# Order of weight splits and query steps in a windowed attention layer

## The chip, the cores and the metric

The kernel runs on one core of one Trainium2 chip. The metric is the device time of one launch in microseconds (us). One core has TensorE (PE: matmuls and transposes; PEld: its weight loads), VectorE (DVE), ScalarE (ACT), GpSimd (POOL), SyncE (SP, which here issues the DMAs), and 16 DMA engines. All engines share an on-chip memory (SBUF); matmuls write to accumulation banks (PSUM).

## The reference, cut to what matters

A network of two blocks on 512 tokens of width 1024: a retention layer, a windowed attention layer, and then a mixer, cross attention and MLP layers. The change lies in the windowed attention layer alone:

```
def swa_layer(x, g_norm, w_in, g_q, sinks, w_out, k_band, v_band, bias, mask):
    proj = rmsnorm(x, g_norm) @ w_in
    q, gate = jnp.split(proj, [SWA_Q_WIDTH], axis=-1)
    q = rmsnorm(q.reshape(b, nb, BLOCK, SWA_KV_HEADS, SWA_GROUP, SWA_HEAD_DIM), g_q)
    scores = jnp.einsum('bnqkgd,bnjkd->bnkgqj', q, k_band).astype(jnp.float32)
    scores = scores * (SWA_HEAD_DIM ** -0.5) + bias[None, None]
    scores = jnp.where(mask[None, :, None, None], scores, -jnp.inf)
    sink = sinks.astype(jnp.float32).reshape(1, 1, SWA_KV_HEADS, SWA_GROUP, 1, 1)
    m = jnp.maximum(jnp.max(scores, axis=-1, keepdims=True), sink)
    p = jnp.exp(scores - m)
    p = p / (jnp.sum(p, axis=-1, keepdims=True) + jnp.exp(sink - m))
    o = jnp.einsum('bnkgqj,bnjkd->bnqkgd', p.astype(v_band.dtype), v_band)
    o = o.reshape(b, s, SWA_Q_WIDTH) * jax.nn.silu(gate)
    return x + o @ w_out
```

There are 16 query heads of 64, two key/value heads, and four blocks of 128 tokens; a block sees itself and the block before it.

## The kernel before

**Precision.** A factor is split into two parts of a reduced matmul type, `hi` (a rounded copy, written by ScalarE) and `lo` (the rest, written by VectorE). A product is three matmuls, hi by hi, hi by lo and lo by hi: `mm3`, lines L257 to L259.

**Weights.** All weight matrices come in chunks of 128 x 2048 numbers (1 MB), in one list (`order`) in which they are used. `load` issues the DMA of one chunk into one of two raw buffers (`wtiles`, L251) and splits it into one of the weight buffers. In this layer one of the three weight buffers is held for the keys (`hold`), so that two take turns: the split of chunk n + 1 overwrites chunk n - 1, and can begin when the matmuls of n - 1 have ended. The chunks of `b_w_in` have a norm's factors worked into the split: eight ScalarE instructions (`split_scaled`, L168) and eight VectorE instructions (L169) of 128 x 256. Other chunks are split by two of each (`split`, L159 and L160). `prefetch(n)` loads until n chunks are ready; `chunk(..., ahead=k)` first calls `prefetch(k + 1)` and then takes the next one, so that `ahead=1` loads the chunk behind the one that is taken, and `ahead=0` loads none beyond it.

**The layer's loop.** The heads go in four groups c = 0 to 3, the queries of c being chunk 2c of `b_w_in` and its gate chunk 2c + 1. `q_part(c)` works in two halves of two blocks (b2 = 0, 1): a projection with 256 columns for each block (96 matmuls over both halves), `normed` (a square on ScalarE at L648, a sum at L650 and L652, a power on GpSimd at L285, the scaling at L656), a split into `qx` (L159, L160), eight transposes by PE (L706), and four ScalarE copies of the transposed queries into `oh` and `ol` (L709; the tiles are called swa_oh and swa_ol in rows). It is a generator with three steps: the first half up to the split; the first half's transposes and copies and the second half up to the split; the second half's transposes and copies. `gate_part(c)` has two steps, one for each 128 columns of the gate, with 24 matmuls of 512 columns each and the `silu_gate`. `attend(c, b, bt)` does the scores of one block (L742: eight matmuls, for which the transposed queries of that block must be there), the bias and the softmax; `values` transposes the probabilities (L772), splits them (pTh, pTl) and multiplies by the values, then by the gate (L782). It runs three blocks behind.

**What sets the order.** The program text gives priorities. A planner works out, before the run and by its own estimate of each instruction's time, the order of the instructions on each engine: among those whose inputs and buffers it takes to be ready, the one that stands first in the text. The queues then run in that order. So an instruction that stands late in the text can be queued early if it is ready early. `tc.issue_after(ins)` adds to all instructions that its block makes on the engine of `ins` the condition that they are queued behind `ins`; it adds no wait, and holds nothing on other engines.

Of the kernel before, what the change touches and what calls it, by code (L numbers as in the profile page):

```python
# [17 lines left out]
P = 128  # L18
# [95 lines left out]
class Net:  # L114
# [503 lines left out]
    def swa(self, after):  # L618
        nc, tc, a = self.nc, self.tc, self.a
# [23 lines left out]
        def normed(ps3, nh, b2):  # L643

            nh = 2 * nh
            sq = self.sp.tile([P, 512], F32, tag="sq", bufs=3, name=self.uid("qs"))[:, :nh * 64].rearrange(
                "p (h d) -> p h d", d=64)
            nc.scalar.activation(sq, ps3, AF.Square)  # L648
            ss = self.sp.tile([P, 32], F32, tag="ss", name=self.uid("ss"))[:, :nh]
            nc.vector.tensor_reduce(out=ss, in_=sq, axis=AX.X, op=ALU.add)  # L650
            sv = ss.rearrange("p (b h) -> p b h", b=2)
            nc.vector.scalar_tensor_tensor(  # L652
                out=sv, in0=sv, scalar=1.0 / 64, op0=ALU.mult, op1=ALU.add,
                in1=self.e1[:, 2 * b2:2 * b2 + 2].unsqueeze(2).to_broadcast([P, 2, nh // 2]))
            r = self.pow_col(ss, nh, 0.0)
            nc.vector.tensor_tensor(out=sq, in0=ps3, in1=r.unsqueeze(2).to_broadcast([P, nh, 64]), op=ALU.mult)  # L656
            return sq

        ck = self.chunk("w_kv", 0, ahead=1)
        for b2 in range(2):  # L660
# [19 lines left out]
            for x in range(2):  # L680
                pt = self.bank("ax").rearrange("p (b g t) -> p b g t", b=2, g=2)
# [8 lines left out]

        def q_part(c):

            ck = self.chunk("b_w_in", 2 * c, ahead=1)
            for b2 in range(2):
                ps = self.bank().rearrange("p (b c) -> p b c", b=2)
                for b in range(2):
                    self.tproj(ck, xs, b2 * 2 + b, ps[:, b, :])
                qn = normed(ps.rearrange("p b (h d) -> p (b h) d", d=64), 4, b2)
                qx = p2.tile([P, 8, 2, 64], F32R, tag="qx", name=self.uid("qx"), bufs=1)
                self.split(qx[:, :, 0], qx[:, :, 1], qn)  # L700
                qf = qx.rearrange("p (b h) x d -> p b h (x d)", b=2).bitcast(F32)
                yield
                for b in range(2):
                    pt = self.bank("ax").rearrange("p (h t) -> p h t", h=4)
                    for h in range(4):
                        nc.tensor.transpose(pt[:, h], qf[:, b, h], ident)  # L706
                    t0 = b2 * HALF + b * P
                    for i, t in enumerate((oh, ol)):
                        nc.scalar.copy(t[:, 2 * c:2 * c + 2, t0:t0 + P], pt[:, 2 * i:2 * i + 2])  # L709
            yield  # L710

        def gate_part(c):
            ck = self.chunk("b_w_in", 2 * c + 1, ahead=1)
            sg = sgs[c] = p2.tile([P, 2, S], F32, tag="sg", name=self.uid("swsg"))
            for j in range(2):
                self.silu_gate(self.proj(ck, j, xs, full), sg[:, j, :], rb)
                yield
# [3 lines left out]
        def bias_load(c):  # L721
            bt = p2.tile([P, 2, 2, 256], F32, tag="bias", name=self.uid("bias"))
            v = self.scr[:]
            for g in range(2):
                src = bass.AP(tensor=v.tensor, offset=v.offset + 127 + (8 * g + 2 * c) * 384,
                              ap=[[16 * 384 - 1, P], [384, 2], [1, 256]])
                nc.sync.dma_start(bt[:, g], src)
            return bt
# [34 lines left out]
        def values(c, b, s, sg):  # L763
            w = P if b == 0 else 256
            nj = w // P
            po = self.bank("ax")[:, :256]
            n = 0
            for g in range(2):
                pt = self.bank("ax").rearrange("p (j t i) -> p j t i", j=2, t=2)
                for t in range(2):  # L770
                    for j in range(nj):
                        nc.tensor.transpose(pt[:, j, t, :], s[:, g, t, j * P:(j + 1) * P], ident)  # L772
                pT = [p2.tile([P, 2, 256], F32R, tag=x, name=self.uid(x)) for x in ("pTh", "pTl")]
                src = pt.rearrange("p j t i -> p j (t i)")
                self.split(pT[0][:, :nj], pT[1][:, :nj], src[:, :nj])
                for j in range(nj):
                    self.mm3(po, [z[:, b + 1 - nj + j, g, :] for z in vz], [x[:, j, :] for x in pT],
                             n == 0, n == 2 * nj - 1)
                    n += 1
            u = self.sp.tile([P, 512], F32, tag="sq", bufs=3, name=self.uid("ou"))[:, :256].rearrange("p (t i) -> p t i", t=2)  # L780
            bs = slice(b * P, (b + 1) * P)
            nc.vector.scalar_tensor_tensor(out=u, in0=sg[:, :, bs], scalar=0.5,  # L782
                                           in1=po.rearrange("p (t i) -> p t i", t=2), op0=ALU.mult, op1=ALU.mult)
            self.split(oh[:, 2 * c:2 * c + 2, bs], ol[:, 2 * c:2 * c + 2, bs], u)

        for _ in q_part(0):
            pass
        prev = []
        for c in range(4):
            bt = bias_load(c)  # L790
            g, q = gate_part(c), q_part(c + 1) if c < 3 else iter([None] * 3)
            fill = [(g, g), (), (q,), (q, q)]
            for b in range(NB):
                s = attend(c, b, bt)
                for x in fill[b]:
                    next(x)
                if len(prev) == 3:
                    values(*prev.pop(0))
                prev.append((c, b, s, sgs[c]))
# [627 lines left out]
```

## Time and profile before

| | us |
|---|---|
| median of 3 runs | 1888.41 |
| lowest, highest | 1884.99, 2663.68 |
| the profiled execution, its own time | 1888.0 |
| its span in the profile | 1886.2 |
| granted TensorE clock, mean | 0.997 |

The span reaches from the first to the last instruction; 1.8 us of the profiled execution lie outside it. The highest of the three runs is far from the two others. Times in rows are microseconds from the start of the span, unless marked ns. "Idle before" is the time for which an engine stood still ahead of an instruction, with what ended it. PEclk is the granted TensorE clock as a share of full speed.

### The profile page before, as it was taken

The numbers are of one execution on the slowest core, as the hardware profiler recorded it, in microseconds if no ns is written. First come the engines' busy times: TensorE is split into PE (matmuls) and PEld (weight loads), VectorE is DVE, ScalarE is ACT, GpSimd is POOL, SyncE is SP. The second block draws the span as 40 slices with busy tenths as digits, with TensorE's granted clock in tenths as the row PEclk, the third lists the DMA queues.
The fourth block names the chain that finished last, engine by engine and source line by source line (L and its number), as shares of the span: only waits on it lengthen the run. The fifth ranks groups of instructions, "written<-read, shape, count | busy, mean of one in ns | idle before, by whom it ended". The sixth has DMA issues, their size and how long they took to land.

```text
span 1886.2 us, 25702 instructions
## 1 busy us (share of the span) xinstructions
PE 1856.7 (98%) x10626; PEld 1627.5 (86%) x10626; DVE 1115.2 (59%) x1942; ACT 721.0 (38%) x1338; POOL 40.2 (2%) x51
## 2 busy tenths in 40 slices
PE   8999999999999999999999999999999999999998
PEld 7888888889888988888998888888899898888886
DVE  5564646567887566647556644444595575444445
ACT  5333223245655344434543423223254353233231
POOL 0000000001110000000000000000000000000000
PEclk9999999999999999999999999999999999999999
DMA  7224222213221322223522432322322133223221
GB/s 266 95 84 151 87 95 68 90 51 109 67 68 56 115 68 68 90 67 112 195 75 70 158 108 89 105 97 90 108 83 68 68 112 123 90 89 112 90 90 45
DMA packets 34038, 182.50 MB, mean 97 GB/s; under 512 B 4033, under 2 KB 8705, under 8 KB 14721
## 3 DMA queue, kind: packets, MB, share of 16 engines
q1 hardware_dynamic: 33920, 180.86, 27.9%
q8 instruction: 83, 1.36, 0.3%
q14 instruction: 35, 0.28, 0.0%
HBM read 178.72 MB, written 5.27 MB: 98 GB/s over the span
## 4 chain that ended last, share of the span: by engine, by line
PE 95%; DVE 3%; ACT 1%; DMA 0%; issue 0%; SPq 0%; DVEq 0%; POOLq 0%; POOL 0%; ACTq 0%
PE mm L257 30%; PE mm L259 30%; PE mm L258 30%; PE ax L325 1%; DVE w L160 1%; PE ax L257 0%; PE ax L293 0%; PE ax L258 0%; PE ax L259 0%; PE ax L772 0%; PE mm L742 0%; PE ax L1091 0%; ACT w L168 0%; PE ax L706 0%; PE mm L1222 0%
## 5 line engine op out<-in xcount | busy, mean ns | idle before, releaser
L257 PE MATMUL mm<-xh,w 128*128 128x512 f32 (+1 forms) x1312 | 462.4, 356 | 7.4 <-ACT xh L168 6.6
L258 PE MATMUL mm<-xl,w 128*128 128x512 f32 (+1 forms) x1312 | 463.5, 354 | 0.0
L259 PE MATMUL mm<-xh,w 128*128 128x512 f32 (+1 forms) x1312 | 463.4, 354 | 0.0
L159 ACT CAST w<-raw 128x1024 fp32r<-128x1024 f32 (+1 forms) x284 | 282.8, 1043 | 436.2 <-PE mm L259 269.5
L160 DVE TENSOR_TENSOR w<-raw,w 128x1024 fp32r<-128x1024 f32 (+1 forms) x284 | 337.0, 1216 | 130.6 <-ACT w L159 130.5
L257 PEld LDWEIGHTS mm<-xh,w 128*128 128x128 f32 x1312 | 246.1, 189 | 42.7 <-ACT xh L168 6.6
L259 PEld LDWEIGHTS mm<-xh,w 128*128 128x128 f32 x1312 | 247.3, 189 | 34.4
L258 PEld LDWEIGHTS mm<-xl,w 128*128 128x128 f32 x1312 | 247.3, 189 | 34.3 <-DVE xl L169 0.3
L381 DVE SCALAR_TENSOR_TENSOR x<-x,mm 128x512 f32<-128x512 f32 x192 | 131.5, 685 | 201.3 <-PE mm L259 201.2
L257 PE MATMUL mm<-w,hh 128*128 128x512 f32 x512 | 199.3, 389 | 0.0
L258 PE MATMUL mm<-w,hh 128*128 128x512 f32 x512 | 199.2, 389 | 0.0
L259 PE MATMUL mm<-w,hl 128*128 128x512 f32 x512 | 199.2, 389 | 0.0
L257 PE MATMUL mm<-w,xh 128*128 128x256 f32 x544 | 153.4, 282 | 0.9 <-ACT xh L159 0.4
L259 PE MATMUL mm<-w,xl 128*128 128x256 f32 x544 | 152.7, 281 | 0.2 <-DVE xl L160 0.2
L258 PE MATMUL mm<-w,xh 128*128 128x256 f32 x544 | 152.3, 280 | 0.0
L258 PEld LDWEIGHTS mm<-w,hh 128*128 128x128 f32 x512 | 96.1, 188 | 20.1
L259 PEld LDWEIGHTS mm<-w,hl 128*128 128x128 f32 x512 | 96.1, 188 | 19.9
L257 PEld LDWEIGHTS mm<-w,hh 128*128 128x128 f32 x512 | 96.1, 188 | 19.8
L257 PEld LDWEIGHTS mm<-w,xh 128*128 128x128 f32 x544 | 102.9, 189 | 3.8 <-ACT pre L914 2.3
L1159 DVE TENSOR_TENSOR rl<-rl 128x512 f32<-128x512 f32 (+1 forms) x72 | 45.1, 631 | 100.6 <-ACT rl L1157 100.6
L259 PEld LDWEIGHTS mm<-w,xl 128*128 128x128 f32 x544 | 102.9, 189 | 0.4 <-DVE xl L160 0.4
L258 PEld LDWEIGHTS mm<-w,xh 128*128 128x128 f32 x544 | 102.6, 189 | 0.2
(343 smaller groups left out, 2829.6 us busy)
## 6 DMA issues: line engine op xcount, KB each, us to landing
raw<-in_mlp_w_dram SPq DMA_DIRECT2D x64, 1024.0 KB, 4.9
raw<-in_a_w_in_dram SPq DMA_DIRECT2D x23, 1024.0 KB, 5.1
raw<-in_ml_w_in_dram SPq DMA_DIRECT2D x12, 1024.0 KB, 5.1
raw<-in_a_w_out_dram SPq DMA_DIRECT2D x8, 1024.0 KB, 5.0
raw<-in_b_w_in_dram SPq DMA_DIRECT2D x8, 1024.0 KB, 4.9
raw<-in_xa_wq_dram SPq DMA_DIRECT2D x8, 1024.0 KB, 4.8
raw<-in_mem_w_kv_dram SPq DMA_DIRECT2D x8, 1024.0 KB, 5.1
raw<-in_xa_wo_dram SPq DMA_DIRECT2D x8, 1024.0 KB, 5.0
```

What stands on the lines that cost most here:

```text
L159: nc.scalar.copy(hi, src)
L160: return nc.vector.tensor_tensor(out=lo, in0=src, in1=hi.bitcast(F32), op=ALU.subtract)
L257: mm(o, a[0], b[0], start=first, stop=False)
L258: mm(o, a[0], b[1], start=False, stop=False)
L259: mm(o, a[1], b[0], start=False, stop=last)
L325: nc.tensor.transpose(ps[:, t * P:(t + 1) * P], self.x[:, b, f:f + P], self.c("ident"))
L381: self.nc.vector.scalar_tensor_tensor(out=x, in0=x, scalar=alpha, in1=ps, op0=ALU.mult, op1=ALU.add, **({} if acc is None else {"accum_out ...
L1159: nc.vector.tensor_tensor(out=u, in0=u, in1=u, op=ALU.mult)
```

## The change

In `q_part` and `gate_part` the chunk is taken with `ahead=0`. The next chunk's load is called later: in `q_part(c)` behind the transposes and copies of the first half (so that the gate's weights of c come there), and in `gate_part(c)` at once (the queries' weights of c + 1), in both cases inside `issue_after` the last copy so far, which `self.evac` keeps. And the three steps of `q_part(c + 1)`, which ran one in block 2 and two in block 3 of group c, run one in each of the blocks 1, 2 and 3.

```
 
         def q_part(c):
 
-            ck = self.chunk("b_w_in", 2 * c, ahead=1)
+            ck = self.chunk("b_w_in", 2 * c, ahead=0)
             for b2 in range(2):
                 ps = self.bank().rearrange("p (b c) -> p b c", b=2)
                 for b in range(2):
...
                     for i, t in enumerate((oh, ol)):
-                        nc.scalar.copy(t[:, 2 * c:2 * c + 2, t0:t0 + P], pt[:, 2 * i:2 * i + 2])
+                        self.evac = nc.scalar.copy(t[:, 2 * c:2 * c + 2, t0:t0 + P], pt[:, 2 * i:2 * i + 2])
+                if b2 == 0:
+                    with tc.issue_after(self.evac.ins):
+                        self.prefetch(1)
             yield
 
         def gate_part(c):
-            ck = self.chunk("b_w_in", 2 * c + 1, ahead=1)
+            ck = self.chunk("b_w_in", 2 * c + 1, ahead=0)
+            with tc.issue_after(self.evac.ins):
+                self.prefetch(1)
             sg = sgs[c] = p2.tile([P, 2, S], F32, tag="sg", name=self.uid("swsg"))
...
             g, q = gate_part(c), q_part(c + 1) if c < 3 else iter([None] * 3)
-            fill = [(g, g), (), (q,), (q, q)]
+            fill = [(g, g), (q,), (q,), (q,)]
             for b in range(NB):
```

## Rows read from the trace of the kernel before

**Rows 1.** The page: the span, and busy time, share and instructions of each engine.

```profile
span 1886.2 us, 25702 instructions
PE 1856.7 (98%) x10626; PEld 1627.5 (86%) x10626; DVE 1115.2 (59%) x1942; ACT 721.0 (38%) x1338; POOL 40.2 (2%) x51
```

**Rows 2.** Windows: length, busy time of each engine (instructions), clock, DMA share, GB/s.

```profile
445.46:587.00 141.54, 130.41 (x883) 118.46 (x882) 115.66 (x288) 90.79 (x272) 11.76 (x7) 0.99 0.20 64
587.00:1886.20 1299.20, 1288.88 (x7224) 1122.97 (x7223) 741.08 (x1234) 468.71 (x794) 17.29 (x28) 1.00 0.28 95
```

**Rows 3.** Who waited for whom, PE alone, from 440 to 640.

```profile
PE mm L742 <- ACT swa_oh L709: 7.0, 3, 2.8
PE ax L772 <- DVE pTl L160: 2.0, 2, 1.0
PE ax L706 <- DVE qx L160: 1.2, 3, 0.6
PE ax L257 <- DVE ou L782: 0.5, 1, 0.5
```

**Rows 4.** Timeline of PE: start, length, instruction, count, idle time before.

```profile
485.02 1.03 PE L706 MATMUL ax<-cst,qx 128*128 128x128 f32 x8
488.83 0.74 PE L742 MATMUL mm<-kT,swa_oh 128*128 128x256 f32 x4 [2.77 <-ACT swa_oh L709]
...
490.88 1.09 PE L706 MATMUL ax<-cst,qx 128*128 128x128 f32 x8 [0.37 <-DVE qx L160]
...
530.28 0.74 PE L742 MATMUL mm<-kT,swa_oh 128*128 128x256 f32 x4 [2.74 <-ACT swa_oh L709]
...
531.80 1.97 PE L706 MATMUL ax<-cst,qx 128*128 128x128 f32 x8 [0.31 <-DVE qx L160]
...
571.32 0.74 PE L742 MATMUL mm<-kT,swa_oh 128*128 128x256 f32 x4 [1.44 <-ACT swa_oh L709]
```

**Rows 5.** Timeline of ACT at the first and the third of these waits.

```profile
485.22 3.30 ACT L168 ACTIVATE w<-raw,vec 128x256 fp32r<-128x256 f32 x8 [2.55 <-PE mm L259]
488.42 0.35 ACT L709 CAST swa_oh<-ax 128x256 fp32r<-128x256 f32 x1
...
569.00 1.99 ACT L159 CAST w<-raw 128x1024 fp32r<-128x1024 f32 x2 [1.12 <-PE mm L259]
570.90 0.36 ACT L709 CAST swa_oh<-ax 128x256 fp32r<-128x256 f32 x1
```

**Rows 6.** Windows behind the second wait, columns as in rows 2.

```profile
532.00:534.00 2.00, 2.00 (x11) 2.00 (x11) 1.16 (x2) 1.36 (x4) 0.00 (x0) 0.50 0.84 328
534.00:536.00 2.00, 2.00 (x15) 2.00 (x15) 0.00 (x0) 0.45 (x2) 0.00 (x0) 0.75 0.34 143
```

**Rows 7.** Timeline of PE: first matmuls of the gate projections of c = 0 and 1.

```profile
445.46 0.39 PE L257 MATMUL mm<-xh,w 128*128 128x512 f32 x1
...
474.14 0.39 PE L257 MATMUL mm<-xh,w 128*128 128x512 f32 x1
```

**Rows 8.** Groups by line, 440 to 600: count, busy us, mean ns, idle before.

```profile
L168 ACT ACTIVATE w<-raw,vec 128x256 fp32r<-128x256 f32 x48 | 19.9, 497 | 3.7 <-PE mm L259 3.7
```

**Rows 9.** The chain that ended last, in order of time: start, length, what.

```profile
459.30 0.95 PE mm L742 x8
460.25 0.87 PE ax L706 x8
```

**Rows 10.** Timeline, c = 0, first half: ACT's square, DVE's end of the split.

```profile
439.23 0.60 ACT L648 ACTIVATE qs<-mm 128x512 f32<-128x512 f32 x1 [0.48 <-PE mm L259]
...
444.11 0.68 DVE L160 TENSOR_TENSOR qx<-qs,qx 128x512 fp32r<-128x512 f32 x1
```

**Rows 11.** The page's DMA issues: count, size of each, median us to landing.

```profile
raw<-in_b_w_in_dram SPq DMA_DIRECT2D x8, 1024.0 KB, 4.9
```

**Rows 12.** Timeline, c = 1, first half: the same two instructions as in rows 10.

```profile
467.80 0.60 ACT L648 ACTIVATE qs<-mm 128x512 f32<-128x512 f32 x1 [3.57 <-PE mm L259]
...
479.90 0.68 DVE L160 TENSOR_TENSOR qx<-qs,qx 128x512 fp32r<-128x512 f32 x1
```

## The prediction

> **What bounds the kernel now.** I began with the page's first part: TensorE (PE) is busy 1856.7 us of 1886.2 us, 98%, the other engines 59% and less [rows 1]. All that an edit of order can win is therefore idle time of PE, 29.5 us in the whole program, and the question is how much of it lies in the stage that is changed. The windows answer that: the attention layer's loop over head groups runs from the end of the first query projection (445.46) to about 587; in these 141.54 us PE is busy 130.41, so 11.1 us are idle. The 1299 us behind it hold 10.3 us of idle time and the work before 445.46 the rest; the edit touches neither [rows 1, 2]. PE's list of waits for this stage gives 10.7 of the 11.1 us names: 7.0 us in three waits of the scores (L742) for ScalarE's copies of the transposed queries (L709), 2.0 us for VectorE's second part of the probabilities, 1.2 us in three waits of the query transposes (L706) for the second part of qx, 0.5 us for the gated output [rows 3].
>
> The timeline of PE shows where the three big waits stand: 2.77 us before 488.83, 2.74 us before 530.28 and 1.44 us before 571.32, that is, once at each change of the head group c. The first comes right behind eight query transposes that began at 485.02 [rows 4]. ScalarE's timeline says why. At 485.22, when the gate projection of c = 1 has freed its weight buffer, ScalarE takes the eight slices of the next weights (3.30 us) and only then the copy at 488.42. The third wait is the same with a plain split, 1.99 us before the copy at 570.90 [rows 5]. So the wait is neither for PE nor for VectorE but for a place in ScalarE's queue, and it is taken there by weights that nobody wants yet: a gate uses them, and a whole query projection, some 11 us, stands in front of that gate.
>
> One more cost hangs on the second wait. From 532 to 534 the granted clock is 0.50 of full (1.2 GHz) and from 534 to 536 it averages 0.75, with PE busy throughout; what PE does before the clock falls is the 2.74 us of waiting. That is 0.50 x 2 + 0.25 x 2 = 1.5 us lost [rows 4, 6]. Eight transposes take 1.97 us there and 1.09 us after the first wait, where the clock stays up [rows 4].
>
> **The change part by part.** Nothing is removed or added in computation; each of the eight input chunks is still loaded by one DMA and split by eight ScalarE and eight VectorE instructions. Two things move.
>
> First, the order of the splits. The gate's weights of group c, up to now free to be split as soon as their buffer is free, come behind the four copies of the first two blocks' queries of the same c; the queries' weights of c + 1 come behind the last copies of group c. The edge binds ScalarE's half; VectorE's half needs ScalarE's result and follows. The gate projection of c, which stood ahead of those copies (at c = 1 it runs from 474.14 to 485.02, 10.9 us, while the queries are still being normed [rows 7]), must now stand behind them, so its buffer can't come free in front of them either. That holds for the third wait too: the split in front of it, the output weights, goes into the buffer of the last gate. All three waits of L742 lose their cause: **-6.95 us**. The qx waits (0.37, and with the other two 1.25 us together [rows 3, 4]) come from the same queue, since the ScalarE half of qx stands behind the same split and copies: **-1.25 us**. The clock's drop, which follows the second wait: **-1.5 us**. The other 2.5 us of [rows 3] are waits for VectorE inside the softmax; I let them stand.
>
> The Trainium skill (TensorE: Matmul & The Clock Gate, "Part 1: The HAM clock gate") says that the slow clock is the default and activity lifts it. The trace agrees at the second wait and not at the first, which is as long and shows no drop. If the drop is tied to the wait, the sum below stands; if it is not, it may fall elsewhere and the sum is 1.5 us smaller.
>
> What the delayed split costs is not in the trace, and I bound it. From the last copy of the first half to the first usable slice of the gate's weights lie one ScalarE and one VectorE slice, about 0.4 us each by 3.30 / 8 [rows 5] and 497 ns as the mean of one [rows 8]: 0.9 us. Each slice then feeds three matmuls of 0.23 us (10.9 us / 48 [rows 7]), 0.69 us a slice, so the split stays ahead. In those 0.9 us PE has the scores of blocks 0 and 1 of that group, 0.95 us each [rows 9], which wait for these copies alone. So the gap is near 0 if the order comes out that way, and 4.2 us (the whole split and VectorE's tail, 3.3 + 0.9) if the planner puts something else first. I take 0.5 us for each of c = 1, 2, 3, near the lower end, as the scores stand ahead of the gate in program order: **+1.5 us**. A gain is excluded here: work is made later, not cheaper.
>
> At c = 0 there is no such cover. The gate projection starts at 445.46, without a wait, on weights split beforehand [rows 7]. After the change it needs the copies first: the VectorE half of qx ends at 444.8, 0.7 us after 444.11 [rows 10], eight transposes take 0.87 us [rows 9], two copies of 0.35 us [rows 5] 0.7 us more, the first slice 0.9 us: 447.3 at best. In between PE has these transposes and as many of the keys', 1.7 us together. Bounds 0 and 4.2 us as above; I take **+1.0 us**, nearer the lower, as the matmuls of two blocks' scores can go in as well.
>
> Second, the queries' three steps go to blocks 1, 2, 3 where they stood at 2, 3, 3. A step more or less in a block costs nothing of itself: the same instructions. It moves the half chain (square, sum, power on GpSimd, scaling, split) up by a block, and its transposes from the group's end into the block before. What hides it is the work of PE in between: the second half's projection (48 matmuls of half the gate's width, some 5.5 us [rows 7]), the scores and the values. The weights of q(c + 1) have the whole gate projection of c to be split in. VectorE is no bound: 115.66 of 141.54 us [rows 2]. On the DMA queue each of the loads goes out later in the order, a 1 MB transfer of 4.9 us [rows 11] into the raw buffer of the chunk two before, and the bias transfer of the next group stands behind it; the raw buffer is free a gate projection (10.9 us) earlier, so I cost both at nothing. Without that cover it would be up to 4.9 us for a chunk. GpSimd's queue holds only the powers, and no load passes it.
>
> Sum: -6.95 - 1.25 - 1.5 + 1.5 + 1.0 = -7.2 us. Against the profiled execution, 1888.0 us, that is **1880.8, say 1881 us**. The shown median is 1888.4, the same within 0.4 us; the two lower runs are 1885.0 and 1888.4, so some 3 us is chance.
>
> **The rivals.** *A, the forecast:* 1881 us, 1877 to 1885.
>
> *B, the waits change their name:* PE loses as much to the softmax chain or to late gate weights as it gains at the copies. For it: the order on every engine is worked out by a planner before the run, and the old trace is already full of matmuls of the gate that filled gaps; tied to the copies, they no longer can. Against: the gate is now free exactly where the softmax of a new group starts. Price: 0, 1888 us, 1885 to 1891.
>
> *C, slower: the gate projection is missed as cover of the queries' chain.* From the square to the second part of qx the chain takes 5.5 us when VectorE is free (439.23 to 444.8 [rows 10]) and 12.8 us in the loop (467.80 to 480.6 [rows 12]). Now the gate waits for the whole of it: 12.8 + 0.87 (transposes) + 1.4 (four copies) + 0.9 (slice) = 16.0 us from the end of the first half's projection. As cover remain 5.5 us of the second half, 1.9 us of scores and some 2.3 us of one block's values (eight transposes and twelve matmuls of 0.12, as 0.95 / 8 [rows 9]): 9.7 us. Uncovered 6.3 us, three times 18.9 us, with a clock drop of 1.5 us each in place of one: 18.9 + 3.0 - 8.2 = +13.7 us, **1902 us**. It decides from a chain of about 6.5 us on. Against it: in the long chain stand the splits that now come later, and the step has a higher place in the order.
>
> *D, all idle time of the stage goes, and the drop:* 1888.0 - 11.1 - 1.5 = 1875 us. For it speaks that each head group then has scores and a gate ready together; against it the 2.5 us that wait for VectorE. That the change leaves the waits of L742 as they were is no case of its own: the edge forbids it.
>
> **How the numbers follow.** A 0.50, B 0.25, C 0.15, D 0.10. The likeliest is A: 1881 us. The range must leave out no more than 2 in 10: it reaches from D (1875, less 1) over A and B to the milder half of C (up to +5 us): 1874 to 1893. Faster and slower by 2% means 38 us, about what a measurement of this kernel can tell from no change; that is over three times all idle time of the stage, and nearly three times C. So within 2%: 0.98; slower 0.01, faster 0.01.
>
> **What the changed profile would show.** If the first step is right, PE's waits show no L742 behind L709 of over 0.7 us, and on ScalarE four copies L709 stand ahead of each eight slices L168. If the cost of the delay is right, PE's waits for the split (L257 to L259 of the gate behind L168 or L169) sum to under 3 us, some of it at c = 0 near 446. If C is right, PE idles 3 us and more before each gate projection, with a clock of 0.50 behind it. If B is right, idle time between 445 and 587 stays near 11 us under other names, DVE pTl first. Wrong altogether would be a shift outside this stage, where I expect the stretch behind it to have its length of before.

## The result: slower by 1.0%, and where the time went

The changed kernel takes 1906.9 us (median of five runs, 1904.32 to 1909.29) against 1887.03 us before (median of five runs by now): a ratio of 1.0102, interval 1.0086 to 1.0119. The run of 2663.68 us before is a slow one and left out of the ratio. That is within 2%, but its sign is clear, and it is the other sign than forecast, outside the range of 1874 to 1893. The profiled execution took 1905.86 us. Its page answers to [rows 1]:

```profile
span 1904.1 us, 25709 instructions
PE 1866.9 (98%) x10626; PEld 1633.7 (86%) x10626; DVE 1117.5 (59%) x1942; ACT 719.7 (38%) x1338; POOL 40.0 (2%) x51
```

TensorE has the same 10626 instructions and is busy 10.2 us longer; it also idles 37.2 us in place of 29.5. The windows, cut where those of [rows 2] were cut, say where:

```profile
445.46:605.00 159.54, 140.70 (x875) 124.65 (x874) 122.07 (x300) 91.22 (x275) 11.78 (x7) 0.94 0.21 70
605.00:1904.10 1299.10, 1288.73 (x7223) 1122.61 (x7221) 739.39 (x1229) 468.29 (x793) 17.14 (x28) 1.00 0.28 95
```

All of it is in the attention layer's loop: 159.54 us in place of 141.54, while what follows has kept its length (1299.10 and 1299.20). The 18.0 us are 7.7 us of idle time (18.8 for 11.1) and 10.3 us of longer busy time. Cut into windows of 2 us from 440 to 640, busy time times the missing share of the granted clock sums to 9.6 us, before to 1.7. So the ledger is **+7.7 us of waits, +7.9 us of slow clock, 2.4 us unassigned**.

The first surprise is in PE's list of waits, 440 to 640 (waiting line, who was waited for, us in total, times, longest):

```profile
PE mm L747 <- ACT swa_oh L709: 5.9, 3, 3.2
PE mm L257 <- ACT w L168: 2.9, 2, 1.4
PE mm L747 <- DVE s L749: 2.2, 2, 1.8
PE ax L706 <- DVE ou L787: 1.6, 2, 1.4
PE ax L257 <- ACT pTh L159: 1.5, 1, 1.5
PE mm L258 <- DVE w L169: 1.4, 2, 0.8
PE mm L747 <- DVE qs L656: 1.1, 1, 1.1
PE ax L258 <- DVE pTl L160: 0.8, 1, 0.8
PE ax L706 <- DVE qx L160: 0.7, 1, 0.7
```

(Each kernel's added lines shift the numbers behind them; here by five, so that L747 is the scores' L742 and L787 the gated output's L782. In the rows of other kernels the tiles tell the operation: mm<-kT,swa_oh are the scores, ax<-cst,s the transposes of the probabilities, ax<-cst,qx those of the queries.) The wait that the change was to remove is still there, 5.9 us for 7.0 in [rows 3], and below it stand new ones: for weights (2.9 + 1.4) and for the gated output `ou` (1.6). PE's timeline gives their places:

```profile
514.24 0.38 PE L258 MATMUL ax<-pTl,vzh 128*128 128x256 f32 x1 [0.84 <-DVE pTl L160]
...
514.93 0.62 PE L706 MATMUL ax<-cst,qx 128*128 128x128 f32 x4
516.96 0.66 PE L706 MATMUL ax<-cst,qx 128*128 128x128 f32 x4 [1.40 <-DVE ou L787]
...
519.63 0.77 PE L257 MATMUL mm<-xh,w 128*128 128x512 f32 x1 [1.44 <-ACT w L168]
...
541.29 0.74 PE L747 MATMUL mm<-kT,swa_oh 128*128 128x256 f32 x4 [3.18 <-ACT swa_oh L709]
...
584.01 0.79 PE L747 MATMUL mm<-kT,swa_oh 128*128 128x256 f32 x2 [2.55 <-ACT swa_oh L709]
```

Compare 514.93 and 516.96 with 485.02 in [rows 4]: there eight transposes were one run, here they are two runs of four, and the second waited 1.40 us for VectorE to have read `ou`. ScalarE's timeline at 517 and at 541 shows what came between the copies:

```profile
516.87 0.35 ACT L709 CAST swa_oh<-ax 128x256 fp32r<-128x256 f32 x1
517.12 0.36 ACT L709 CAST swa_ol<-ax 128x256 fp32r<-128x256 f32 x1
517.39 3.30 ACT L168 ACTIVATE w<-raw,vec 128x256 fp32r<-128x256 f32 x8
...
520.98 0.36 ACT L709 CAST swa_oh<-ax 128x256 fp32r<-128x256 f32 x1
...
536.32 0.37 ACT L709 CAST swa_oh<-ax 128x256 fp32r<-128x256 f32 x1 [2.29 <-PE ax L706]
536.58 0.38 ACT L709 CAST swa_ol<-ax 128x256 fp32r<-128x256 f32 x1
536.85 1.31 ACT L168 ACTIVATE w<-raw,vec 128x256 fp32r<-128x256 f32 x3
538.06 0.40 ACT L159 CAST swa_oh<-ou 128x256 fp32r<-128x256 f32 x1
538.35 2.11 ACT L168 ACTIVATE w<-raw,vec 128x256 fp32r<-128x256 f32 x5
540.36 0.62 ACT L595 ACTIVATE swsg<-g 128x512 f32<-128x512 f32 x1
540.88 0.36 ACT L709 CAST swa_oh<-ax 128x256 fp32r<-128x256 f32 x1
```

Two copies, the eight slices of the split, then the two other copies, as in [rows 5] but with the split in the middle. Which copies these are is told by the planned order of ScalarE's queue (the numbers of tiles rise in the order of the text; `ax_539` is the bank of the block that stands first in the text, `ax_540` of the second; "..." stands for two instructions of the softmax and the values):

```
L709 CAST swa_oh_3660<-ax_540_4530 128x2x128
L709 CAST swa_ol_3661<-ax_540_4530 128x2x128
L168 ACTIVATE w_542_4539<-raw_541_4537,vec_79 128x256 x8
...
L709 CAST swa_oh_3660<-ax_539_4523 128x2x128
L709 CAST swa_ol_3661<-ax_539_4523 128x2x128
```

The second block comes first. `issue_after` was given the copy that is last in the text; that copy is queued first, so the split is queued "behind the copies" and still in front of the other two. The same order stands at four places of the loop: both halves of the queries of c = 2 (517 and 536) and of c = 3 (563 and 580). The two long waits, 3.18 and 2.55 us, stand behind the second halves.

The clock is the other half of the loss. Windows of PE behind these places (length, busy time, granted clock, DMA share, GB/s):

```profile
518.00:526.00 8.00, 6.56 (x18) 0.57 0.38 128
582.00:590.00 8.00, 5.90 (x26) 0.61 0.37 131
542.00:546.00 4.00, 4.00 (x24) 0.60 0.79 264
```

In [rows 6] 4 us ran at 0.50 and 0.75; now there are these three stretches and a fourth from 594 to 598, and each begins at a wait or a row of waits: 0.84, 1.40 and 1.44 us within 6 us up to 519.63, then 3.18, 2.55, and for the fourth the 1.8 us for `s`. The gate's matmuls behind 519.63 follow each other every 0.43 us, at full clock every 0.23 (10.9 us for 48 of them, as the prediction took it from [rows 7]).

### The profile page after: what moved, and what is told of

It is laid out like the page before. It is cut to its first block, busy times and chain, and to the rows that moved or that the text cites. A ratio compares the mean times of both kernels' runs of the same rounds, so it can differ in the third digit from the quotient of the medians.

```text
span 1904.1 us, 25709 instructions
## 1 busy us (share of the span) xinstructions
PE 1866.9 (98%) x10626; PEld 1633.7 (86%) x10626; DVE 1117.5 (59%) x1942; ACT 719.7 (38%) x1338; POOL 40.0 (2%) x51
## 4 chain that ended last, share of the span: by engine, by line
PE 93%; DVE 4%; ACT 2%; DMA 0%; issue 0%; POOL 0%; SPq 0%; DVEq 0%; POOLq 0%; ACTq 0%
PE mm L257 29%; PE mm L259 29%; PE mm L258 29%; PE ax L325 1%; PE mm L747 1%; DVE w L160 1%; PE ax L257 1%; PE ax L259 1%; PE ax L258 0%; PE ax L777 0%; PE ax L293 0%; ACT s L759 0%; ACT w L168 0%; DVE s L749 0%; PE ax L1096 0%
```

## The experiments

The theory after the result: **the edge names the wrong copy** because the blocks are queued in reverse, and they are reversed because the first block's transposes take the bank of the values' output, which is read late (three "ax" banks go round). Rivals: **lost cover**, the prediction's rival C (the gate can no longer fill the time of the queries' chain, and weights come late); and **the steps** themselves cost time, which the prediction had put at nothing. The times are medians, each with the ratio to the kernel before on the same chip; idle time and clock loss are of the stage, 440 to 640, from windows of 2 us. The kernel before has 11.1 and 1.7 there, the changed one 18.8 and 9.6.

| kernel | median us | ratio, 95% | idle | clock |
|---|---|---|---|---|
| edges alone | 1896.74 | 1.0047, 1.0031 to 1.0063 | 15.4 | 4.4 |
| gate's weights tied alone | 1898.90 | 1.0065, 1.0044 to 1.0086 | 16.7 | 4.8 |
| queries' weights tied alone | 1897.75 | 1.0055, 1.0038 to 1.0072 | 14.0 | 4.3 |
| steps alone | 1899.24 | 1.0061, 1.0046 to 1.0076 | 17.7 | 9.0 |
| steps, bank freed early | 1901.90 | 1.0077, 1.0061 to 1.0094 | 18.6 | 5.6 |
| all, behind both blocks | 1899.25 | 1.0061, 1.0041 to 1.0081 | 15.4 | 2.9 |
| all, other banks for transposes | 1898.65 | 1.0055, 1.0038 to 1.0072 | 16.4 | 8.7 |
| all, values' bank last | 1893.51 | 1.0035, 1.0023 to 1.0047 | 13.2 | 3.0 |
| gate's weights behind the previous group | 1884.30 | 0.9986, 0.9977 to 0.9995 | 9.0 | 0.0 |
| previous group + steps | 1895.92 | 1.0044, 1.0029 to 1.0059 | 15.7 | 8.9 |
| previous group + bank last | 1880.73 | 0.9964, 0.9952 to 0.9977 | 6.4 | 1.6 |
| previous group + bank last + steps | 1885.72 | 0.9987, 0.9978 to 0.9995 | 9.2 | 3.1 |
| before + bank last | 1879.95 | 0.9954, 0.9940 to 0.9967 | 6.0 | 1.7 |

**Edges alone**: the changed kernel with the steps where they were.

```
-            fill = [(g, g), (q,), (q,), (q,)]
+            fill = [(g, g), (), (q,), (q, q)]
```

> Only the first part of the change: the splits behind the copies, the queries' steps where they were (one in block 2, two in block 3). Theory L (late block: the last copy in the text is not the last one queued, and the split stands in front of the other block's copies): both steps then run in one block and the same PSUM banks are short, so the waits of L742 for L709 stay above 4 us in sum, and the time is 1900 us or more. Theory G (lost cover: a gate that is tied to the copies can't fill PE's gaps while the queries are normed): the chain of the queries has one block less to hide in, idle time from 445 to 610 rises to 20 us or more, time 1905 to 1915. If the moved steps are the cause, this kernel is at 1888 or below.

Measured: +0.47%. From PE's waits, 440 to 640:

```profile
PE ax L706 <- DVE qx L160: 3.6, 1, 3.6
PE ax L258 <- DVE pTl L160: 2.4, 3, 2.1
...
PE mm L258 <- DVE w L169: 2.2, 2, 1.2
PE mm L257 <- ACT w L168: 2.0, 2, 1.0
...
PE mm L747 <- ACT swa_oh L709: 0.2, 1, 0.2
```

Here 0.2 us of waits for the copies are left in place of 7.0, and the kernel is slower all the same; neither theory had expected that (over 4 us of these waits, or 20 us of idle time and more). The price stands above it: 4.2 us for weights that are split late, and 3.6 us at 480.93 for `qx`, with no gate ready to fill the time. The first halves of c = 2 and 3 are queued in reverse here too (at c = 2 copies at 519.84, the split at 520.37, the other block's copies at 530.04), but PE has a gate projection to do between the two blocks. The second halves, where the changed kernel waits longest, are transposed in one run each (534.46 and 574.90): only with the moved steps do they come apart. So the reversed blocks explain the changed kernel's 5.9 us, not its sign.

**Steps alone**: the kernel before with the new `fill` and nothing else.

> Only the second part: the queries' steps in blocks 1, 2, 3, the weights split as soon as their buffer is free. Theories L and G both put the loss on the first part and expect no loss here: 1880 to 1890 us. If the moved steps are the cause, 1900 us or more.

Measured: +0.61%, more than the edges, from a list that adds no instruction. Its waits:

```profile
PE mm L742 <- ACT swa_oh L709: 5.9, 2, 3.1
PE mm L257 <- DVE qs L656: 5.4, 1, 5.4
PE ax L258 <- DVE pTl L160: 3.0, 2, 2.4
```

The gate of c = 2 waits 5.37 us, ahead of 518.22, for VectorE's scaling (L656), which reads the second half's projection out of the bank that this gate projection needs; the first matmuls behind it run every 0.43 to 0.56 us. "A step more or less in a block costs nothing of itself" is refuted: the steps take banks, and a bank is held until a chain of ScalarE, GpSimd and VectorE has read it. The two parts together cost 0.47 + 0.61 = 1.08%, the whole change 1.02%: they add up, though through other waits than each has by itself.

**Is it that bank?** Steps alone, with the queries' half copied out of the bank by ScalarE at once:

```
-                qn = normed(ps.rearrange("p b (h d) -> p (b h) d", d=64), 4, b2)
+                qs = self.sp.tile([P, 512], F32, tag="sq", bufs=3, name=self.uid("qc"))
+                nc.scalar.copy(qs.rearrange("p (b c) -> p b c", b=2), ps)
+                qn = normed(qs.rearrange("p (h d) -> p h d", d=64), 4, b2)
```

> The steps in blocks 1, 2, 3 alone, with each half of the queries copied from PSUM to SBUF by ScalarE (0.6 us) before it is normed, so that its bank is free for the gate. In the kernel with the steps alone PE waited 5.4 us for the scaling of the queries, which is the last to read that bank, and lost some 3 us more to the clock behind it. Theory P (the moved steps change whose PSUM bank the gate takes over): that wait goes, time 1889 to 1893. Rival (the steps themselves starve PE): PE waits as long under another name, 1897 or more.

Measured: +0.77%, no better than without the copy. The wait changed its owner:

```profile
PE mm L744 <- ACT swa_oh L711: 7.7, 3, 3.1
PE mm L257 <- ACT qc L699: 7.1, 2, 3.6
```

ScalarE's copy is itself queued late (PE waits 3.65 us for it ahead of 515.61 and 3.42 ahead of 563.08): at the first place behind the softmax, eight slices of the next weights (3.4 us from 510.88) and a part of `qx`, at the second behind the softmax and a part of `qx`. So the bank came free no earlier by having a reader on another engine: that reader has a place in a queue as well.

**One edge at a time.** The kernel before with the edge and `ahead=0` in `q_part` only (the gate's weights of c behind the first half's copies of c):

> The first part's first half alone: the gate's weights of c behind the copies of the first half of the queries of c; the queries' weights as before; steps as before. Theory G (lost cover by the gate): nearly all of the loss of the first part, 1893 to 1899. If the queries' weights carry it, 1886 to 1890.

and with those in `gate_part` only (the queries' weights of c + 1 behind the copies of c):

> The first part's second half alone: the queries' weights of c + 1 behind the last copies of c; the gate's weights as before; steps as before. Theory G: the gate still fills PE's gaps, the waits for the copies at the group's change stay (7 us, since the gate's split is what stands in front), time 1886 to 1891. If late queries' weights are what costs, PE waits for L168 or L169 by 3 us and more and the time is 1892 or more.

Measured: +0.65% and +0.55%, and the two together, +0.47%, cost no more than either. The gate's edge alone shows what rival C had described, from PE's timeline:

```profile
486.40 1.97 PE L706 MATMUL ax<-cst,qx 128*128 128x128 f32 x8 [6.50 <-DVE qx L160]
```

PE has finished the second half's projection at 479.9 and has nothing until 486.40, since the gate that used to fill this time [rows 7] is tied behind the very transposes that are waited for; then eight transposes run in 1.97 us in place of 1.03, at half clock. The prediction had put this at 6.3 us. It happens once (the only other wait of the kind is 0.3 us), and at c = 0 the scores wait 2.92 us ahead of 450.05. The queries' edge alone leaves 5.8 us of waits for copies, 2.35 of it ahead of 463.30: its split is behind the copies, but the gate's free one is queued ahead of them. Its time is that of the second forecast (late queries' weights, 1892 us or more), but PE's waits for weights come to 1.2 us and not to 3; of its 10 us of loss the two columns of the table show 5.5, and the rest is open.

**Behind both blocks.** The changed kernel with the split behind the last copy of each of the two blocks, whichever is queued last:

```
-                    with tc.issue_after(self.evac.ins):
+                    with tc.issue_after(self.evacs[0]), tc.issue_after(self.evacs[1]):
```

> The changed kernel, with the splits queued behind the last copies of both blocks and not only behind the copy that is last in the text. Theory L: waits of the scores for L709 fall from 5.9 us to under 2 us, the clock drops behind them (near 542 and 584) go, time about 1895. Theory G: the split comes still later, the waits take the name of L168 (2.9 us before, 5 us or more now), time 1905 or more.

Measured: +0.61%, 0.4% better than the change. This is the direct test of the named copy: waits for the copies fall from 5.9 to 1.5 us, and the slow stretches at 518 and 542 are gone; only one from 582 to 590 is left.

```profile
PE mm L749 <- ACT swa_oh L710: 1.5, 3, 0.7
```

What stays is the 1.9 us for `ou` and a dozen other entries of 0.3 to 2.0 us, for weights, probabilities and `qs` among others.

**Other banks for the queries' transposes**: taken from the five "mm" banks, out of the values' way.

```
-                    pt = self.bank("ax").rearrange("p (h t) -> p h t", h=4)
+                    pt = self.bank().rearrange("p (h t) -> p h t", h=4)
```

> The changed kernel, with the transposed queries in the ring of five PSUM banks that the projections use and not in the ring of three that the values use. Theory L: the transposes of the first block no longer wait for the values' output (1.6 us for ou in the changed kernel, 0 here), all four copies stand together ahead of the split, the scores' waits for L709 fall under 2 us; with both waits gone the time is 1885 to 1895. Theory G: the copies come earlier by at most 2 us a group, the gate still waits for its split, time 1898 or more.

Measured: +0.55%. The copies' waits go (0.4 us), `ou` goes from PE's list, and one takes their place:

```profile
PE mm L257 <- DVE qs L656: 9.7, 4, 3.2
```

**The values' bank last.** In the changed kernel `values` takes its output bank `po` behind the banks of its two transposes, not in front of them; the queries' transposes then meet a bank that is freed early.

```
+            pts = [self.bank("ax").rearrange("p (j t i) -> p j t i", j=2, t=2) for _ in range(2)]
             po = self.bank("ax")[:, :256]
...
-                pt = self.bank("ax").rearrange("p (j t i) -> p j t i", j=2, t=2)
+                pt = pts[g]
```

> The changed kernel, with the values' output taking its PSUM bank after the two banks of its transposes and not before them, so that the first block's query transposes take over a bank that is free early. Theory L: no wait of L706 for ou (1.6 us before), the copies come in the order of the text and the split behind all four; the waits for L709 (5.9 us) and the clock drops at 542 and 584 go: 1890 to 1897. If the loss is all lost cover, 1900 or more.

Measured: 1893.51 us, +0.35%, some 13 us better than the change by this alone. The copies stand in the order of the text again, all eight transposes in one run, L706 waits for `ou` no more and the scores wait 0.2 us for the copies:

```profile
513.43 1.04 PE L706 MATMUL ax<-cst,qx 128*128 128x128 f32 x8
```

```profile
PE mm L747 <- ACT swa_oh L709: 0.2, 1, 0.2
```

So the late bank is the cause of the reversed blocks. It is not the cause of most of the loss: by the same edit the kernel before gets faster too, by 0.46% (further down), so that of the 0.67% won here only some 0.2% belongs to the change. The kernel still is 0.35% slower than the one before; the largest waits left are weights (1.8 us), `ou` at other places (3.5) and `pTl` (2.9).

**The same aim without lost cover.** The kernel before, with each group's gate weights queued behind all copies of the *previous* group, and the output weights behind those of the last; steps as before.

```
+            behind(c - 1, 2)
             ck = self.chunk("b_w_in", 2 * c, ahead=1)
...
-                        nc.scalar.copy(t[:, 2 * c:2 * c + 2, t0:t0 + P], pt[:, 2 * i:2 * i + 2])
+                        e = nc.scalar.copy(t[:, 2 * c:2 * c + 2, t0:t0 + P], pt[:, 2 * i:2 * i + 2])
+                    self.done[c].append(e.ins)
```

> The kernel before, with the gate's weights of group c queued behind all copies of the queries of c - 1 (and the output weights behind those of c = 3), not behind those of its own group; steps as before. This takes the split out of the copies' way and leaves the gate free to be hoisted. If the 7 us of waits for the copies are a plain place in ScalarE's queue, they fall to under 1.5 us and the time to 1877 to 1882 with the clock drop gone. If any new order gives the idle time back elsewhere, 1886 or more.

Measured: 1884.30 us, between the two forecasts, a ratio of 0.9986 with its interval just below 1. All waits for the copies are gone and so is all clock loss of the stage, as the prediction had wanted. But this is the whole list of waits:

```profile
PE mm L752 <- DVE s L754: 2.6, 4, 0.8
PE ax L782 <- DVE pTl L160: 2.6, 2, 1.4
PE ax L258 <- DVE pTl L160: 2.5, 2, 1.9
PE mm L257 <- DVE s L754: 0.8, 1, 0.8
PE ax L715 <- DVE qx L160: 0.4, 1, 0.4
```

7.0 us of waits for ScalarE became 8.5 us for VectorE in the softmax, where [rows 3] have 2.0: the prediction's rival B, the waits change their name.

**The steps once more**, on top of that:

> The kernel of the run before with the gate's weights behind the previous group's copies (1884 us), and the queries' steps moved to blocks 1, 2, 3. The moved steps alone cost 12 us in the kernel before, where they kept the waits for the copies. If what they cost is a bank that the gate takes over from the second half of the queries, the wait of PE for the scaling L656 (5.4 us there) appears again and the time is 1893 to 1900. If they cost only through the copies' place in the queue, 1885 or less.

Measured: +0.44% against the kernel before, 0.58% above the same without the new steps. The chief wait is another one than for steps alone, the values' transposes for the bank of the query copies:

```profile
PE ax L782 <- ACT swa_ol L718: 5.4, 2, 3.2
```

**Both cures.** The previous group's weights and the values' bank last:

> The gate's weights behind the previous group's copies, steps as before, and the values' output bank last. If the late bank also costs there (the first block's transposes at 526 and 568 stood behind a whole gate projection), the scores of block 0 come 10 us earlier and the softmax waits shrink: 1878 to 1883. If PE is filled by the gate meanwhile, it is worth nothing: 1883 to 1886.

The kernel before with the values' bank last alone:

> The kernel before with the values' output bank last, nothing else. If the place in ScalarE's queue and the late bank are two causes, the waits for L709 stay near 7 us here and the time is 1883 to 1888; if the late bank alone made the copies late, they go and it is at 1881 like the run that has both edits.

Measured: 1880.73 and 1879.95 us, ratios 0.9964 and 0.9954, whose intervals overlap: the best two, and the second changes two lines and moves no weight and no step. The second's forecast had 7 us of waits for the copies or none; 3.9 us are left. It also splits the prediction's three waits. From its timeline, and the windows behind:

```profile
488.40 0.74 PE L742 MATMUL mm<-kT,swa_oh 128*128 128x256 f32 x4 [2.77 <-ACT swa_oh L709]
```

```profile
490.00:492.00 2.00, 2.00 (x10) 0.50 0.78 311
492.00:494.00 2.00, 2.00 (x14) 0.69 0.36 152
```

The first wait of [rows 4] is unchanged to the hundredth, the second (2.74 us ahead of 530.28) is gone, the third is 1.10 us for 1.44. In the kernel before, the four transposes of one block stand at 514.35 and those of the other at 526.48, behind a gate projection; here at 518.62 and 520.59. So only the first and most of the third hung on the split's place in ScalarE's queue alone; the second hung on the late bank as well.

**And the steps on both cures:**

> The best version so far (gate's weights behind the previous group's copies, output bank last, 1881 us) with the queries' steps moved to blocks 1, 2, 3. Moved steps cost 12 us in the kernel before and 12 us in the run with the edges alone. If they cost because query transposes and values take over each other's PSUM banks, most of that is gone here: 1880 to 1886. If the earlier query projection itself leaves PE short of work later in the group, 1890 or more.

Measured: 1885.72 us, 0.9987 where the same kernel without the new steps has 0.9964. With the bank last the steps cost 0.23%, some 4 us, and not 0.6%. The longest wait left is again one for `ou`, with a granted clock of 0.50 from 514 to 520 behind it. PE's last matmul for it begins at 510.42; VectorE computes `ou` at 513.60, behind four slices of the next weights and the scaling of the softmax:

```profile
514.06 1.12 PE L783 MATMUL ax<-cst,s 128*128 128x128 f32 x4 [3.37 <-DVE ou L793]
```

## Why the prediction was wrong

The sum was -7.2 us, and the stage became 18.0 us longer. Its terms one by one:

**"All three waits of L742 lose their cause: -6.95 us."** Failed in the changed kernel, where 5.9 us remain. "The edge forbids it", said of the case that the waits stay, is the sentence that was wrong: the edge holds the split behind one copy, and with the blocks reversed that is the copy queued first. The long waits stand where the moved steps, the change's other part, reverse the second halves as well. Shown by binding it to both blocks (1.5 us left) and by undoing the reversal (0.2). It could have been asked beforehand: the edge names an instruction by its place in the text, and the queues of this kernel don't follow the text.

**The value of those waits.** This step failed by more. Where they do vanish (edges alone, previous group), the idle time of the stage goes to 15.4 and 9.0 us from 11.1, not to about 4. The prediction read PE's list of waits as if each could be taken out by itself; the previous group's kernel has 0 us in that line and 6.5 us more in VectorE's. Its ratio, 0.9986, is rival B's, and that was the fair forecast for an edit that does what this one meant to do.

**"+1.5 us" for the delayed split, "+1.0" at c = 0.** The first was mis-sized: the gates of c = 2 and 3 wait 2.9 us for their weights (1.44 ahead of 519.63, 1.43 ahead of 565.64) in the changed kernel, and with the gate's edge alone the lost cover is 6.50 us, as rival C had it with 6.3, once and not three times. The second was too high: at c = 0 PE waits 0.15 us ahead of 446.48 for the copies, and not for the gate's weights. But 1.4 us ahead of 463.81 and 466.39 go to the next queries' weights, which had "the whole gate projection of c to be split in" and were put at nothing. Rival C had the right sign and nearly the time (1902 for 1906.9) but as a whole it isn't what happened: in the changed kernel L706 waits 0.7 us for `qx`, where the edges alone have 3.6. The steps, which come a block earlier, give back cover that the edges lose, and have a price of their own.

**"A step more or less in a block costs nothing of itself."** Failed: +0.61% alone, 0.58% and 0.23% on two other kernels, 11.5 to 4 us. Work was not added, but the banks of the next queries are taken a block earlier, between banks of the values that are read late. The prediction had named the cover (PE's work, the weights' time, the DMA queue) and left out PSUM. That the bank order is most of the price is shown on one base only (0.58% without the bank last, 0.23% with it); other banks for the transposes gave 9.7 us of waits for `qs` in its place. The DMA and GpSimd parts held as far as PE's waits go, none of which names either; behind them ScalarE waits 1.76 us ahead of 589.26 for the output weights' transfer, and in steps alone the power on GpSimd takes 2.20 us of the chain that PE waits 5.37 us for.

**The clock, "-1.5 us".** Right in kind, wrong in sign: the stage loses 9.6 us to it in place of 1.7. The rule drawn from one row, that the fall follows a wait, held in each of the four stretches, though not every wait brought a fall; nothing in the sum priced new waits at wait plus clock, although rival C did.

**What held.** The stretch behind the stage kept its length. Of the -1.25 us for the qx waits less than half came: 0.7 us are left. ScalarE's split, at 3.30 us, has the place in the queue that makes the first wait: bound behind the copies (previous group) it takes the wait away, and with the bank last alone the wait stays. That idle time and not work is at stake held too, if the clock that it costs is counted with it.

**What stays open.** 2.4 us of the changed kernel's longer busy time are in neither account. With the values' bank last the changed kernel takes 1.0035 of the kernel before where the latter takes 0.9954; of these 0.8%, 0.23% may be the steps, by the last run, and the rest would be the edges, whose price on that base was not run by itself. Nor was the later call of the load (`ahead=0`) run without the edge around it: what the edges cost is the price of both. In edges alone and with the gate's edge alone no split waits for its transfer, so a late transfer is not what it is there.

## What to carry to other kernels

An order edge is worth what its instruction's place in the queue is: bind to every instruction that must come first, and look at the planned queue before counting the gain; where two equal blocks are queued against the text, ask which buffer the first one waits for. Don't tie work behind a chain that it has been covering: splits tied to the previous group's copies cost nothing (0.9986), tied to their own group's some 9 us. And when steps are moved, list the PSUM banks that they take and who reads those last: here the order of three allocations in `values`, which the prediction never named, was worth 0.46%, a larger gain than any edit of weights or steps brought by itself.

## What was not expected of the hardware

In the changed kernel the granted clock that fell cost as much as the added waits: 7.9 us beside 7.7. And the same wait may or may not bring a fall: 2.77 us ahead of 488.83 in the kernel before left the clock at 1.00 from 486 to 496, 2.77 us ahead of 488.40 with the values' bank last was followed by 0.50 and 0.69, with the same eight transposes in front of it. In the changed kernel three shorter waits within 6 us (0.84, 1.40 and 1.44) were followed by 0.57 over 8 us. What decides between the two cases of 2.77 us the traces don't show.
